# Two feed-forward networks in seven products: a stream of its own for the input combinations, and three plain tiles in the first network

## The chip, the cores and the metric

The kernel runs on one core of a Trainium2 chip. The metric is the device time of one execution in microseconds (us). The median of several runs is taken; lower is better. The engines are PE (TensorE, matmuls; PEld is its weight load), DVE (VectorE), ACT (ScalarE), POOL (GpSimd) and SP (SyncE, which here issues the transfers). Each runs its own instructions in a fixed order and waits on semaphores for the others.

## The reference, cut to what matters

A first block (a retention layer and a differential attention layer on 512 tokens of width 1024) is followed by a second one with two gated feed-forward networks of hidden width 2816 around a mixing layer. The change touches the two feed-forward networks only:

```python
def swiglu(x, w_gate, w_up, w_down):
    return (jax.nn.silu(x @ w_gate) * (x @ w_up)) @ w_down
...
def second_block(x, meta_tokens, ffn1_norm, ffn1_w_gate, ...):
    h = jnp.concatenate([meta, x], axis=1)          # 16 + 512 tokens
    for l in range(DEPTH_2):                        # DEPTH_2 = 1
        h = h + 0.5 * swiglu(rmsnorm_2(h, ffn1_norm[l]), ffn1_w_gate[l], ffn1_w_up[l], ffn1_w_down[l])
        u = rmsnorm_2(h, mix_norm[l])
        ...
        h = h + merged @ w_out[l]
        h = h + 0.5 * swiglu(rmsnorm_2(h, ffn2_norm[l]), ffn2_w_gate[l], ffn2_w_up[l], ffn2_w_down[l])
    return rmsnorm_2(h, final_norm)[:, N_META:]
```

The gain of the norm and the division by the root of the mean square are separate in the kernel: the matmuls take the input times the gain, and the factor of each token (called `bc`) is multiplied in afterwards.

## The kernel before, in words

All activations lie transposed in SBUF: `h[0..7]` are eight tiles of 128 channels by the tokens (528 in the first network, which also has 16 meta tokens; 512 in the second). Every float32 operand of a matmul is split into a rounded high part and a rest (`xh`, `xl`, `wh`, `wl`: ACT casts the high part, DVE subtracts it from the source), and every product is three matmuls, high by high, high by rest and rest by high (`mm3`).

A hidden tile is 128 of the 2816 hidden channels; there are 22 (`FT`). A tile needs a gate product and an up product, each over eight channel tiles. **Plain products** (tile 0 and 1, `FS` = 2) take the weights one tile `[128, 1024]` at a time from a stream (`plan`, then `raws`, two raw buffers, then `ready`; `stock` and `w`), three split pairs `wh`/`wl` at most. In the first network a plain gate or up tile is 48 matmuls of 264 columns (two token halves in two PSUM banks), so a plain hidden tile is 96.

**Seven products** (`Seven`, all other tiles) take a gate tile and an up tile together: split by halves of the channels they are a 2 by 2 matrix of blocks, the input split by halves of channels and tokens is another, and the 2 by 2 product is done with seven block products in place of eight. A block product is 12 matmuls (four channel tiles, three matmuls each), so a hidden tile is 84. For this there must be sums of weight blocks (`sums`, two on POOL and two on DVE per tile, from float32 copies that `load` fetches), splits of the seven weight operands (`split`, one half of a `wh`/`wl` pair each), and **combinations of the inputs**. `inputs` makes three of them once for each network: for each of four channel tiles ACT makes one product into a temporary (`e` in the first network, `o` in the second) and three casts, and DVE three combinations into the temporary and three rests into tiles named `at`; together 24 instructions on DVE and 16 on ACT. `first` overwrites the second token half of `x[0..3]` with a fourth combination just before the seven products start.

The program is recorded by generators (`Ctx.run`), which take turns by a model of time. Operations of DVE, ACT, POOL and SP are held back (`ops`) and written out per engine by earliest modelled start (`pump`), ties broken by rank; the matmuls stand in the order in which the generators make them. What comes out is one fixed order per engine. Two generators run in a network. `backbone` makes the matmuls: first the gate of tile 0, the up and the gate (three weight tiles), then the up of tile 1, then the seven products, then the down products (`wd`). `stats` closes the norm of the layer before (`arrive`), sums the squares, makes the token factor (matmul `pst`, DVE `rsv`, POOL power `rsr`, DVE `diag`, matmul `pbc`, ACT copy `bc`), finishes tile 0 and the gate of tile 1 (`up(0, ...)`, `R["t1"]`: DVE multiplies by `bc` into `t`, ACT applies Silu, DVE multiplies by the up product `mm`, both split into `hh`), and only then runs `seven.inputs`, with a rank that is three higher. `seven.feed` makes the loads, sums and splits of the next weight operands when there is room, from the up of tile 1 on. There are six PSUM banks for products (`mm`, taken in a ring), so the seventh bank wanted is free when the operation that reads the first is done: the banks of the up of tile 0 are read by `t<-mm,t`.

Of the kernel before, what the change touches and what calls it, by code (L numbers as in the profile page):

```python
# [11 lines left out]
F32R = mybir.dt.float32r  # L12
# [6 lines left out]
P = 128  # L19
D = 1024  # L20
KT = D // P
# [686 lines left out]

FS = 2


def ffn_items(which):
    it = []
    for f in range(FS):
        it += [(f"wg{which}", f, 0, 1024, None), (f"wu{which}", f, 0, 1024, None)]
    it.append(None)
    for m in range(KT):
        it += [(f"wd{which}", m, j * P, min(8, FT - j) * P, None) for j in range(0, FT, 8)]  # L720
    return it


class Seven:
# [9 lines left out]
    def __init__(self, c, which, pool, psp, entry, o, TH):  # L734
        self.c, self.which, self.pool, self.psp, self.entry, self.o, self.TH = c, which, pool, psp, entry, o, TH
        self.x = entry.x
        self.blocks = []
        for f in range(FS, FT + 1):
            for k, g in ((1, f), (4, f - 1), (2, f), (6, f), (3, f - 1), (7, f), (5, f)):
                if FS <= g < FT:  # L740
                    self.blocks.append((g, k))
        acts = [("load", FS), ("sums", FS)]
        for f, k in self.blocks:
            acts.append(("split", f, k))
            if (k == 4 or f == FS and k == 1) and f + 2 - (k == 1) < FT:
                acts.append(("load", f + 2 - (k == 1)))
            if k == 5 and f + 1 < FT:
                acts.append(("sums", f + 1))
        self.acts = acts
        self.g, self.u, self.a, self.ops, self.T = {}, {}, {}, {}, {}  # L750
        self.pair, self.made, self.used = None, 0, 0


    def at(self, j, shape, dtype):
        return self.pool.tile(shape, dtype, tag="more" if j == FT else f"hh{j}", name=self.c.nm("at"))

    def rank(self, f):
        c = self.c
# [9 lines left out]
    def feed(self):  # L768
        c = self.c
        while self.acts:  # L770
            it = self.acts[0]
            if it[0] == "load" and c.raws:
                return
            if it[0] == "split" and self.made % 2 == 0 and len(c.ready) + c.live + self.live() >= 3:
                return
            self.acts.pop(0)
            self.rank(lambda: getattr(self, it[0])(*it[1:]))
# [132 lines left out]
def ffn(c, which, after=None, out=None):  # L910
# [7 lines left out]
    with ExitStack() as es:  # L918
# [17 lines left out]
        def stats():  # L936
# [7 lines left out]
            yield from c.wait(lambda: c.rdy(R["bc"]) if "ps" in R else None)  # L944
            up(0, gate([R["t0"][:, i] for i in range(nb)]), R["ps"][1])
            R["t1"] = gate(R["ps"][2])
            c.mark(("first",))
            c.rank += 3
            yield from seven.inputs(temps)
            R["inputs"] = True  # L950

# [33 lines left out]
        def halve(*fs):  # L985
            for f in fs:
                h = pool.tile([P, W], F32R, tag=f"hh{f}", name=c.nm("hh"))
                l = pool.tile([P, W], F32R, tag=f"hl{f - 1}" if f > FS else "more", name=c.nm("hh"))
                c.split(h, l, hid[f])
                hh[f] = h, l  # L990


        def done(f, k, s):
            if not s.acts and c.plan and c.plan[0] is None:
                c.plan.pop(0)
                s.rank(lambda: halve(*range(2, 10)))
            if not s.acts:
                c.stock(s.live())
            if f == FT - 1 and k in (6, 7, 4):
# [5 lines left out]
        def backbone():  # L1005
# [26 lines left out]
                        c.stock(n - 1 - j)  # L1032
            R["ps"] = ps
            t = None
            for f in range(1, FS):
                if f > 1:
                    pg = MM()
                    yield from steps(pg, c.w(wg, f), x)
                    t = gate(pg)
                pu = MM()  # L1040
                w = c.w(wu, f)
# [46 lines left out]

        last = Final(c, pool, psp, out)
        if out is not None:  # L1090
            c.run(last.close(0), last.close(1), stats(), backbone())
            return
        c.run(stats(), backbone())


HR, DK, DV = 8, 128, 256
# [1741 lines left out]
```

## Time and profile before

| | |
|---|---|
| median of 3 runs | 2061.24 us (2056.95 to 2061.69) |
| the profiled execution's own time | 2056.42 us, span 2054.4 us |
| mean granted TensorE clock | 0.983 of full speed |
| PE busy | 1966.2 us (96%), 12509 matmuls |
| DVE, ACT, POOL busy | 1395.5, 981.1, 557.5 us |

The span is from the first to the last instruction; the execution's own time is a little more. The profile cuts the span in 40 slices of 51.4 us. PE is busy 8 tenths or more in all of them but slice 16, where the first network starts (7 tenths, the only slice whose granted clock reads 8 tenths and not 9); the second network starts in slice 34 (8 tenths between slices of 9). PE's row over time and the stretches around these two places are what there is to read.

### The profile page before, as it was taken

Reading aid. Unit: us, or ns where it says so; the run is one execution under the profiler, and the core shown is the slowest. Engines: PE = TensorE matmul, PEld = TensorE weight load, DVE = VectorE, ACT = ScalarE, POOL = GpSimd, SP = SyncE. Lnnn points to the kernel's source line nnn. Section 1 sums busy time; section 2 is a strip of 40 time slices with the busy share of each in tenths; the row PEclk is TensorE's granted clock in tenths of the full one; section 3 lists DMA queues with packets and bytes.
Section 4 is the critical chain, followed back from the end, with each engine's and each line's share of the span. In section 5 each row is a group of like instructions: output and inputs, shape, how many; then the busy total and the mean of one; then the engine's idle time right before and its main releaser. Section 6 shows DMA issues by size and latency. Waiting matters only on the chain. (4 is left out here: it accounts for less than half of the span.)

```text
span 2054.4 us, 32590 instructions
## 1 busy us (share of the span) xinstructions
PE 1966.2 (96%) x12509; PEld 1740.0 (85%) x12509; DVE 1395.5 (68%) x2736; ACT 981.1 (48%) x1987; POOL 557.5 (27%) x457
## 2 busy tenths in 40 slices
PE   8999999989999997999999989999999998999998
PEld 6888888877887886999999988976878787999887
DVE  6665564387677658999833476769786658999733
ACT  4444443256555555555622376643433345555521
POOL 3111120144443153222101243324544231222010
PEclk9999999999999998999999999999999999999999
DMA  4222221322111221333233411021021842333232
GB/s 158 74 82 83 77 78 62 123 72 72 62 63 62 72 83 47 108 100 109 78 94 95 154 47 37 32 83 61 32 73 33 271 153 67 109 116 101 82 98 78
DMA packets 67500, 178.80 MB, mean 87 GB/s; under 512 B 9040, under 2 KB 12240, under 8 KB 67344
## 3 DMA queue, kind: packets, MB, share of 16 engines
q1 hardware_dynamic: 65968, 175.54, 26.2%
q8 instruction: 98, 1.61, 0.3%
q10 hardware_dynamic: 1376, 1.18, 0.2%
q14 instruction: 58, 0.48, 0.1%
HBM read 166.21 MB, written 10.49 MB: 86 GB/s over the span
## 5 line engine op out<-in xcount | busy, mean ns | idle before, releaser
L415 PE MATMUL mm<-x,wh 128*128 128x264 f32 (+2 forms) x2896 | 701.1, 331 | 31.6 <-ACT x L254 15.2
L415 PEld LDWEIGHTS mm<-x,wh 128*128 128x128 f32 x2896 | 487.0, 192 | 75.7 <-ACT x L254 16.2
L415 PE MATMUL mm<-x,wl 128*128 128x264 f32 (+2 forms) x1448 | 476.3, 330 | 18.3 <-DVE wl L254 18.2
L254 ACT CAST wh<-raw 128x1024 fp32r<-128x1024 f32 (+2 forms) x307 | 271.4, 885 | 384.0 <-PE mm L415 244.1
L254 DVE TENSOR_TENSOR wl<-raw,wh 128x1024 fp32r<-128x1024 f32 (+2 forms) x265 | 271.7, 1025 | 184.6 <-ACT wh L254 183.4
L415 PEld LDWEIGHTS mm<-x,wl 128*128 128x128 f32 x1448 | 278.3, 193 | 41.0 <-DVE wl L254 19.2
L415 PE MATMUL mm<-hh,wh 128*128 128x264 f32 (+2 forms) x1100 | 227.0, 315 | 1.5 <-DVE hh L254 1.5
L254 POOL TENSOR_TENSOR acc<-acc,sq 128x512 f32<-128x512 f32 (+4 forms) x73 | 81.3, 1115 | 386.3 <-ACT sq L254 371.7
L415 PEld LDWEIGHTS mm<-hh,wh 128*128 128x128 f32 x1100 | 168.9, 188 | 17.5 <-DVE hh L254 4.4
L415 PE MATMUL mm<-at,wh 128*128 128x264 f32 (+1 forms) x960 | 178.6, 283 | 0.0
L415 PE MATMUL pvg<-wh,x 128*128 128x512 f32 x512 | 170.7, 397 | 0.0
L254 DVE TENSOR_TENSOR wl<-at,wh 128x512 fp32r<-128x512 f32 x200 | 157.0, 794 | 15.3 <-ACT wh L254 12.8
L254 ACT CAST wh<-at 128x512 fp32r<-128x512 f32 x200 | 120.0, 620 | 80.0 <-PE mm L415 70.7
L415 PEld LDWEIGHTS mm<-at,wh 128*128 128x128 f32 x960 | 149.1, 189 | 0.1
L415 PE MATMUL mm<-hh,wl 128*128 128x264 f32 (+2 forms) x550 | 144.6, 315 | 0.0
L415 PE MATMUL mm<-at,wl 128*128 128x264 f32 (+1 forms) x480 | 135.9, 283 | 0.8 <-DVE wl L254 0.8
L254 POOL TENSOR_TENSOR at<-at,raw 128x512 f32<-128x512 f32 x40 | 53.6, 1341 | 288.7 <-DVE wl L254 260.3
L254 POOL TENSOR_TENSOR wl<-raw,wh 128x1024 fp32r<-128x1024 f32 x42 | 101.6, 2422 | 108.1 <-ACT wh L254 102.9
L254 POOL TENSOR_TENSOR ra<-ra,rb 128x512 f32<-128x512 f32 x32 | 57.5, 1798 | 253.5 <-DVE rb L254 253.5
L415 PEld LDWEIGHTS pvg<-wh,x 128*128 128x128 f32 x512 | 96.3, 188 | 20.6
L415 PE MATMUL pvg<-wl,x 128*128 128x512 f32 x256 | 100.4, 392 | 0.0
L415 PEld LDWEIGHTS mm<-hh,wl 128*128 128x128 f32 x550 | 92.0, 188 | 5.5
(441 smaller groups left out, 3769.8 us busy)
## 6 DMA issues: line engine op xcount, KB each, us to landing
raw<-in_wg_dram SPq DMA_DIRECT2D x44, 512.0 KB, 4.1
at<-in_wu_dram SPq DMA_DIRECT2D x80, 256.0 KB, 3.1
raw<-in_w_mix_dram SPq DMA_DIRECT2D x36, 512.0 KB, 3.3
raw<-in_w_ret_vg_dram SPq DMA_DIRECT2D x32, 512.0 KB, 3.3
raw<-in_wd_dram SPq DMA_DIRECT2D x32, 512.0 KB, 3.6
raw<-in_w_dif_kq_dram SPq DMA_DIRECT2D x16, 512.0 KB, 3.2
raw<-in_w_ret_qk_dram SPq DMA_DIRECT2D x14, 512.0 KB, 3.3
raw<-in_w_ret_o_dram SPq DMA_DIRECT2D x13, 512.0 KB, 3.5
```

The lines of the kernel that those rows point to most:

```text
L254: p = Op(lambda: f(*a, **k), self.key, cost, tail, i, o, c.before(o), c.rank, c.t)
L415: return self.nc.tensor.matmul(out, lhsT, rhs, start=start, stop=stop, **kw)
```

## The change

`FS` becomes a number for each network: three plain tiles in the first (so tile 2 is made by plain products, and seven products make 19 tiles there), two as before in the second. `seven.inputs` leaves `stats` and becomes a generator of its own, `inputs`, between `stats` and `backbone` in the order of turns and of ranks. In the first network it starts when the token factor has been recorded as far as its tile `bc`, in the second when the inputs are there. The loads of the float32 weight copies after the first wait until `stats` is done with its part (`later`). The buffer that held a weight sum or copy in the place of tile 2's hidden values is, in the first network, that of the norm's sum (`acc`).

```diff
--- before.py
+++ after.py
@@ -708,12 +708,12 @@
 
 
 
-FS = 2
+FS = {1: 3, 2: 2}
 
 
 def ffn_items(which):
     it = []
-    for f in range(FS):
+    for f in range(FS[which]):
         it += [(f"wg{which}", f, 0, 1024, None), (f"wu{which}", f, 0, 1024, None)]
     it.append(None)
     for m in range(KT):
@@ -734,15 +734,19 @@
     def __init__(self, c, which, pool, psp, entry, o, TH):
         self.c, self.which, self.pool, self.psp, self.entry, self.o, self.TH = c, which, pool, psp, entry, o, TH
         self.x = entry.x
+
+        self.acc = "acc" if FS[which] > 2 else "hh2"
+        self.later = False
         self.blocks = []
-        for f in range(FS, FT + 1):
+        F0 = FS[which]
+        for f in range(F0, FT + 1):
             for k, g in ((1, f), (4, f - 1), (2, f), (6, f), (3, f - 1), (7, f), (5, f)):
-                if FS <= g < FT:
+                if F0 <= g < FT:
                     self.blocks.append((g, k))
-        acts = [("load", FS), ("sums", FS)]
+        acts = [("load", F0), ("sums", F0)]
         for f, k in self.blocks:
             acts.append(("split", f, k))
-            if (k == 4 or f == FS and k == 1) and f + 2 - (k == 1) < FT:
+            if (k == 4 or f == F0 and k == 1) and f + 2 - (k == 1) < FT:
                 acts.append(("load", f + 2 - (k == 1)))
             if k == 5 and f + 1 < FT:
                 acts.append(("sums", f + 1))
@@ -752,7 +756,7 @@
 
 
     def at(self, j, shape, dtype):
-        return self.pool.tile(shape, dtype, tag="more" if j == FT else f"hh{j}", name=self.c.nm("at"))
+        return self.pool.tile(shape, dtype, tag="more" if j == FT else self.acc if j == 2 else f"hh{j}", name=self.c.nm("at"))
 
     def rank(self, f):
         c = self.c
@@ -769,7 +773,7 @@
         c = self.c
         while self.acts:
             it = self.acts[0]
-            if it[0] == "load" and c.raws:
+            if it[0] == "load" and (c.raws or it[1] > FS[self.which] and not self.later):
                 return
             if it[0] == "split" and self.made % 2 == 0 and len(c.ready) + c.live + self.live() >= 3:
                 return
@@ -944,8 +948,12 @@
             yield from c.wait(lambda: c.rdy(R["bc"]) if "ps" in R else None)
             up(0, gate([R["t0"][:, i] for i in range(nb)]), R["ps"][1])
             R["t1"] = gate(R["ps"][2])
+            seven.later = True
             c.mark(("first",))
-            c.rank += 3
+
+        def inputs():
+            for k in range(KT):
+                yield from c.wait(lambda: entry.rdy(k), lambda: 0.0 if "bc" in R or not rest else None)
             yield from seven.inputs(temps)
             R["inputs"] = True
 
@@ -985,7 +993,7 @@
         def halve(*fs):
             for f in fs:
                 h = pool.tile([P, W], F32R, tag=f"hh{f}", name=c.nm("hh"))
-                l = pool.tile([P, W], F32R, tag=f"hl{f - 1}" if f > FS else "more", name=c.nm("hh"))
+                l = pool.tile([P, W], F32R, tag=f"hl{f - 1}" if f > FS[which] else "more", name=c.nm("hh"))
                 c.split(h, l, hid[f])
                 hh[f] = h, l
 
@@ -993,7 +1001,7 @@
         def done(f, k, s):
             if not s.acts and c.plan and c.plan[0] is None:
                 c.plan.pop(0)
-                s.rank(lambda: halve(*range(2, 10)))
+                s.rank(lambda: halve(*range(FS[which], 10)))
             if not s.acts:
                 c.stock(s.live())
             if f == FT - 1 and k in (6, 7, 4):
@@ -1032,10 +1040,13 @@
                         c.stock(n - 1 - j)
             R["ps"] = ps
             t = None
-            for f in range(1, FS):
+            for f in range(1, FS[which]):
                 if f > 1:
                     pg = MM()
-                    yield from steps(pg, c.w(wg, f), x)
+                    w = c.w(wg, f)
+                    for y in steps(pg, w, x):
+                        seven.feed()
+                        yield y
                     t = gate(pg)
                 pu = MM()
                 w = c.w(wu, f)
@@ -1088,9 +1099,9 @@
 
         last = Final(c, pool, psp, out)
         if out is not None:
-            c.run(last.close(0), last.close(1), stats(), backbone())
+            c.run(last.close(0), last.close(1), stats(), inputs(), backbone())
             return
-        c.run(stats(), backbone())
+        c.run(stats(), inputs(), backbone())
 
 
 HR, DK, DV = 8, 128, 256
```

In the program that comes out the first network has 12 more matmuls (one hidden tile of 84 in seven products is now 96), and DVE, ACT, POOL and SP have 9, 8, 2 and 1 instructions fewer. The order changes in two places, the starts of the two networks, and a little where the seven products of the first end.

PE, first network, where the up of tile 1 ends (`wl_7289` before, `wl_7291` now, are the rests of its weights; `x_...` are the split inputs, `mm_...` the banks). Before:

```order
L415 MATMUL mm_7321<-x_6978,wl_7289 128x264
L415 MATMUL mm_7322<-x_6978,wl_7289 128x264
L415 MATMUL mm_7454<-x_6964,wh_7330 128x264
L415 MATMUL mm_7454<-x_6965,wh_7330 128x264
L415 MATMUL mm_7454<-x_6964,wl_7331 128x264
```

Now:

```order
L415 MATMUL mm_7346<-x_6978,wl_7291 128x264
L415 MATMUL mm_7347<-x_6978,wl_7291 128x264
L415 MATMUL mm_7456<-x_6964,wh_7334 128x264
L415 MATMUL mm_7457<-x_6964,wh_7334 128x264
L415 MATMUL mm_7456<-x_6965,wh_7334 128x264
L415 MATMUL mm_7457<-x_6965,wh_7334 128x264
L415 MATMUL mm_7456<-x_6964,wl_7335 128x264
L415 MATMUL mm_7457<-x_6964,wl_7335 128x264
```

Before, the first of the seven products follows, with a half-width weight operand split from `raw_7323`; now the gate of tile 2 follows, in two banks, with the weights `wh_7334` and `wl_7335`, and after it the up of tile 2.

DVE, first network, from the last `diag` of the token factor (before) and from the first combinations behind the `diag`s (now). `e` and `at` are temporaries and results of `inputs`, `t` and `hh` belong to tile 0 and tile 1. Before:

```order
L254 TENSOR_SCALAR diag_7312<-ident,rsr_7301 128x128
L254 TENSOR_TENSOR at_7327<-at_7326,raw_7323 128x512
L254 TENSOR_TENSOR at_7329<-at_7327,raw_7323 128x512
L254 TENSOR_TENSOR wl_7331<-raw_7323,wh_7330 128x512
L254 TENSOR_TENSOR t_7411<-t_1366_7287,bc_7307 128x264 x2
L254 TENSOR_TENSOR t_7411<-mm_7061,t_7411 128x264
L254 TENSOR_TENSOR t_7411<-mm_7062,t_7411 128x264
L254 TENSOR_TENSOR t_7414<-mm_7063,bc_7307 128x264
L254 TENSOR_TENSOR t_7414<-mm_7064,bc_7307 128x264
L254 SCALAR_TENSOR_TENSOR e_7428<-h_84,par,e_7428 128x264
L254 SCALAR_TENSOR_TENSOR e_7427<-h_83,par,e_7427 128x264
L254 TENSOR_TENSOR hh_7413<-t_7411,hh_7412 128x528
```

Now:

```order
L254 SCALAR_TENSOR_TENSOR at_7327<-e_7329,at_7325 128x264
L254 SCALAR_TENSOR_TENSOR e_7331<-h_84,par,e_7331 128x264
L254 TENSOR_TENSOR at_7323<-e_7331,at_7321 128x264
L254 SCALAR_TENSOR_TENSOR at_7319<-e_7331,at_7317 128x264
L254 SCALAR_TENSOR_TENSOR e_7332<-h_85,par,e_7332 128x264
L254 SCALAR_TENSOR_TENSOR at_7327<-e_7331,at_7325 128x264
L254 TENSOR_TENSOR t_7441<-t_1367_7289,bc_7310 128x264 x2
L254 TENSOR_TENSOR t_7441<-mm_7063,t_7441 128x264
L254 TENSOR_TENSOR t_7441<-mm_7064,t_7441 128x264
L254 TENSOR_TENSOR wl_7335<-raw_7008,wh_7334 128x1024
L254 TENSOR_TENSOR hh_7443<-t_7441,hh_7442 128x528
L254 TENSOR_TENSOR t_7444<-mm_7065,bc_7310 128x264
```

Before, two weight sums, a rest and then the finishing of tile 0 followed the `diag`s, and the combinations came behind and among it; now nine combinations stand between the `diag`s and the finishing of tile 0 (four more stand ahead of the `diag`s), the rest `wl_7335` of the gate of tile 2 stands right behind the two `t<-mm,t`, and the other eleven combinations come after.

DVE, second network, around the rest of the weight operands of the first two of the seven products (`wl_17796` before, `wl_17837` now, one half each; `o` is the temporary of `inputs` and of `first`, `x` a result of `first`). Before:

```order
L254 SCALAR_TENSOR_TENSOR at_17817<-o_17819,at_17815 128x256
L254 TENSOR_TENSOR at_17794<-at_17792,raw_17788 128x512
L254 TENSOR_TENSOR x_17421<-o_17880,x_17420 128x256
L254 SCALAR_TENSOR_TENSOR o_17823<-h_17464,par,o_17823 128x256
L254 TENSOR_TENSOR wl_17796<-raw_17788,wh_17795 128x512
L254 SCALAR_TENSOR_TENSOR o_17823<-h_17333,par,o_17823 128x256
L254 TENSOR_TENSOR at_17814<-o_17823,at_17812 128x256
L254 SCALAR_TENSOR_TENSOR o_17823<-h_17464,par,o_17823 128x256
L254 SCALAR_TENSOR_TENSOR at_17810<-o_17823,at_17808 128x256
L254 SCALAR_TENSOR_TENSOR o_17882<-h_17334,par,o_17882 128x256
L254 SCALAR_TENSOR_TENSOR at_17818<-o_17823,at_17816 128x256
L254 TENSOR_TENSOR wl_17796<-raw_17788,wh_17795 128x512
```

Now:

```order
L254 TENSOR_TENSOR t_17839<-mm_17664,t_17839 128x512
L254 TENSOR_TENSOR hh_17841<-t_17839,hh_17840 128x512
L254 TENSOR_TENSOR at_17833<-at_17832,raw_17829 128x512
L254 TENSOR_TENSOR wl_17837<-raw_17829,wh_17836 128x512
L254 TENSOR_TENSOR t_17842<-mm_17828,t_17842 128x512
L254 SCALAR_TENSOR_TENSOR o_17892<-h_17316,par,o_17892 128x256
L254 SCALAR_TENSOR_TENSOR o_17893<-h_17317,par,o_17893 128x256
L254 TENSOR_TENSOR at_17835<-at_17833,raw_17829 128x512
L254 TENSOR_TENSOR hh_17889<-t_17842,hh_17888 128x512
L254 TENSOR_TENSOR x_17364<-o_17892,x_17363 128x256
L254 TENSOR_TENSOR x_17406<-o_17893,x_17405 128x256
L254 TENSOR_TENSOR wl_17837<-raw_17829,wh_17836 128x512
```

Before, the two halves stood among combinations; now all 24 combinations stand ahead of `t_17839`, and between the halves stand the product for tile 1 (`t_17842<-mm_17828`, which reads the last plain matmul's bank), half of `first`, a weight sum and a split.

## Rows read from the trace of the kernel before

**Rows 1.** The page's head and its first part: busy time, share, instructions
```profile
span 2054.4 us, 32590 instructions
...
PE 1966.2 (96%) x12509; PEld 1740.0 (85%) x12509; DVE 1395.5 (68%) x2736; ACT 981.1 (48%) x1987; POOL 557.5 (27%) x457
```
**Rows 2.** Busy time by stretch (first three: first network; last: second)
```profile
780.00:790.00 10.00, 7.24 (x56) 6.57 (x54) 7.75 (x18) 7.54 (x15) 1.56 (x2) 1.00 0.11 38
790.00:800.00 10.00, 1.79 (x8) 1.79 (x9) 10.00 (x26) 6.57 (x17) 0.00 (x0) 0.66 0.08 25
800.00:820.00 20.00, 16.18 (x103) 15.50 (x103) 17.58 (x29) 8.83 (x20) 6.55 (x4) 0.83 0.20 67
1710.00:1720.00 10.00, 3.50 (x15) 3.34 (x16) 9.49 (x24) 7.65 (x20) 0.00 (x0) 0.57 0.00 1
```
**Rows 3.** PE in order of time, first network (start, length, what, idle before)
```profile
784.88 0.41 PE L415 MATMUL mm<-x,wl 128*128 128x264 f32 x2
787.54 0.51 PE L415 MATMUL mm<-x,wh 128*128 128x264 f32 x2 [2.25 <-DVE t L254]
...
798.21 0.59 PE L415 MATMUL mm<-x,wl 128*128 128x264 f32 x1 [8.70 <-DVE wl L254]
...
813.89 0.40 PE L415 MATMUL mm<-at,wh 128*128 128x264 f32 x2
```
**Rows 4.** DVE in order of time, first network
```profile
776.38 1.22 DVE L254 TENSOR_TENSOR wl<-raw,wh 128x1024 fp32r<-128x1024 f32 x1 [1.96 <-ACT wh L254]
...
779.09 3.13 DVE L254 TENSOR_SCALAR diag<-ident,rsr 16x16 f32<-16x16 f32 x5 [1.36 <-POOL rsr L254]
782.15 1.40 DVE L254 TENSOR_TENSOR at<-at,raw 128x512 f32<-128x512 f32 x2
...
787.05 0.77 DVE L254 TENSOR_TENSOR t<-mm,t 128x264 f32<-128x264 f32 x2 [2.21 <-ACT t L254]
...
792.37 1.69 DVE L254 SCALAR_TENSOR_TENSOR e<-h,par,e 128x264 f32<-128x264 f32 x4
...
797.47 0.68 DVE L254 TENSOR_TENSOR wl<-raw,wh 128x512 fp32r<-128x512 f32 x1
```
**Rows 5.** PE in order of time, second network
```profile
1708.63 0.39 PE L415 MATMUL mm<-x,wh 128*128 128x256 f32 x2
1716.50 0.58 PE L415 MATMUL mm<-x,wl 128*128 128x256 f32 x1 [7.47 <-DVE wl L254]
...
1729.10 0.40 PE L415 MATMUL mm<-at,wh 128*128 128x256 f32 x2
```
**Rows 6.** DVE in order of time, second network
```profile
1687.74 1.56 DVE L254 TENSOR_TENSOR wl<-raw,wh 128x1024 fp32r<-128x1024 f32 x1 [0.70 <-ACT wh L254]
...
1691.00 1.91 DVE L254 TENSOR_SCALAR diag<-ident,rsr 128x128 f32<-128x128 f32 x4 [1.13 <-POOL rsr L254]
...
1703.29 0.69 DVE L254 TENSOR_TENSOR t<-mm,bc 128x512 f32<-128x512 f32 x1 [7.54 <-PE mm L415]
...
1708.83 0.69 DVE L254 TENSOR_TENSOR t<-mm,t 128x512 f32<-128x512 f32 x1 [0.47 <-PE mm L415]
```
**Rows 7.** PE, end of the seven-product stretch of the first network
```profile
1009.78 0.66 PE L415 MATMUL mm<-hh,wh 128*128 128x264 f32 x4
```
**Rows 8.** Busy time by stretch, steady part of the second network
```profile
1740.00:1800.00 60.00, 60.00 (x511) 60.00 (x511) 57.87 (x92) 32.65 (x66) 16.90 (x13) 1.00 0.34 109
```
**Rows 9.** ACT in order of time, first network
```profile
785.08 1.28 ACT L254 ACT_TABLE_LOAD   x1
786.38 0.64 ACT L254 ACTIVATE t<-t 128x528 f32<-128x528 f32 x1
```
**Rows 10.** Weight transfers issued in the first network, issue to landing
```profile
DMA to landing us min/median/max: 3.3/3.4/4.8
```
**Rows 11.** PE before the change's places: an idle piece
```profile
749.18 0.59 PE L415 MATMUL mm<-x,wh 128*128 128x264 f32 x1 [2.48 <-ACT x L254]
```
**Rows 12.** Busy time by stretch behind that piece (PEclk: granted clock)
```profile
749.00:759.00 10.00, 9.54 (x45) 9.24 (x46) 7.40 (x15) 5.85 (x15) 6.68 (x8) 0.50 0.46 154
```

## The prediction

> **What bounds the kernel now.** I read the page's first part, then the busy time by stretch, then PE and DVE in order of time where PE's share falls. PE is busy 96% of the span [rows 1], so time can come from few places. Two of them are the starts of the feed-forward networks. From 790 to 800 PE is busy 1.79 of 10 us while DVE is busy all 10, and from 1710 to 1720 PE 3.50 and DVE 9.49 [rows 2]. The reader should see there that PE waits for a DVE that is full, not for a transfer.
>
> First network: the up of tile 1 ends at 784.88 + 0.41 = 785.29. The first of the seven products waits 2.25 us for a bank (its releaser is the DVE product `t<-mm,t`), and the second one 8.70 us for the rest `wl` of its weights; the seventh block product starts at 813.89 [rows 3]. On DVE that `wl` came at 797.47, behind the combinations of `inputs`, such as the four of 1.69 us at 792.37 [rows 4].
>
> Second network: PE comes to the seven products at 1708.63 without a wait, then waits 7.47 us for a `wl`, and starts the seventh block product at 1729.10 [rows 5]. DVE had been idle for 7.54 us ahead of 1703.29 and began the combinations only after that [rows 6].
>
> What each start costs, in one number: from the seventh block product (813.89) to the first down product (1009.78, [rows 7]) PE makes 20 tiles less six blocks, 20 x 84 - 72 = 1608 matmuls, 195.89 us, 0.1218 us each, without an idle piece in PE's rows. Six blocks are then 72 x 0.1218 = 8.77 us, and the first network loses 813.89 - 785.29 - 8.77 = 19.8 us. In the second, 511 matmuls take 60 us [rows 8], a block of 12 is 1.41, and the loss is 1729.10 - 1708.63 - 6 x 1.41 = 12.0 us. Together 31.8 us is all that the change could touch.
>
> **The change part by part.**
>
> *The plain tile.* 96 matmuls for 84: +12 x 0.1218 = +1.46 us on PE. The plain tile is 96 x 0.1218 = 11.69 us of matmuls that need no combinations; one seven-product tile (10.23 us) falls away later, and with it a tile's DVE and ACT work, which lies beside PE and is worth nothing.
>
> *First network, the wait ahead of the gate of tile 2.* Its banks are those that `t<-mm,t` reads, and its `wl` stands right behind that pair on DVE. A combination into the temporary is priced at 1.69 / 4 = 0.42, a rest or any other 264-column pair at 0.77 / 2 = 0.39 [rows 4]. Four combinations ahead of the `diag`s take 3 x 0.42 + 0.39 = 1.65 us where DVE was idle 1.36 for POOL's power: the `diag`s end 0.3 later, at 779.09 + 3.13 + 0.3 = 782.5. Nine combinations follow, 4 x 0.42 + 5 x 0.39 = 3.6, to 786.1; the pair of `t<-t,bc` 0.77, to 786.9 (it ended before 785.08 so far). Then ACT's table load 1.28 and Silu 0.64 [rows 9], the pair `t<-mm,t` 0.77, the `wl` 1.22: 790.8. The first four matmuls of the gate (0.49) don't need the `wl`, so PE loses 790.8 - 0.49 - 785.29 = 5.0 us. From below: if the table load is done before `t` is there, 1.9 less, 3.1. From above: the casts and combinations call each other back and forth between ACT and DVE, and nine steps at some 0.5 us of idleness each add 4.5. I take 5.0, since DVE ran such a mixture from 790 to 800 without idling [rows 2].
>
> *The wait ahead of the up of tile 2.* DVE from 790.8: a split 0.70 (two 264-column halves, priced as 0.77 at most), a `t` pair 0.77, the next ten combinations 5 x 0.42 + 5 x 0.39 = 4.05, the `wl` 1.22: 797.5. The gate's 48 matmuls end at 785.29 + 5.0 + 5.85 = 796.1, and the `wl` is wanted at 796.6: 0.9 us of wait, 0 to 5 by the same two reasons. Ahead of one of the casts ACT must also wait for the weights of tile 3, a transfer that cannot start before the `wl` of 790.8 frees its buffer; it lands 3.4 us later (4.8 at most, [rows 10]), before 796, so it is hidden. If it were slower, the `wl` would be late by as much.
>
> *The first seven products.* The up of tile 2 ends at 796.1 + 0.9 + 5.85 = 802.9. From 797.5 DVE has one rest 0.39, two pairs 1.54, two weight sums of 1.40 / 2 [rows 4], a split 0.70 and two `wl` of 0.68: 5.4 us, to 802.9. So they are there just as PE arrives; 0.5 us for what follows (`first` stands among the next operands), 0 to 3.
>
> *The clock.* Behind an idle piece of 2.48 us [rows 11] PE ran 10 us at a granted clock of 0.50, the 1.2 GHz level [rows 12]; behind the 2.25 us wait at 785 it kept the full level until the 8.70 us wait. After 5.0 us of waiting I expect the low level. The Trainium skill (TensorE: Matmul & The Clock Gate, "HAM oscillation") says the same, that idle gaps bring the clock down and work brings it back; the trace agrees. The loss is half of the slow stretch: 4.9 us if as long as in [rows 12], nothing if the clock holds. Part of it covers the 0.9 us wait and lets DVE get ahead. I take 2.0.
>
> First network: lost 5.0 + 0.9 + 0.5 + 2.0 = 8.4 instead of 19.8, and +1.46: a gain of 10.0 us.
>
> *Second network.* From the end of the gate's `wl` (1687.74 + 1.56 = 1689.3, [rows 6]) DVE now has 24 combinations, 12 x 0.42 + 12 x 0.39 = 9.7, the `diag`s 1.91 and one `wl` of 1.22: 12.9 us, to 1702.2, ahead of the 1703.29 at which it must be free for tile 1. So the combinations are hidden under the plain products, and if ACT makes them 2 us longer, there are still 5 us until the first seven products want anything. But the second half of their first weight operand stands behind `t<-mm,t` for tile 1, which waits for PE's last plain matmul and started at 1708.83: 0.69 + two temporaries 0.84 + sum 0.70 + split 0.69 + two rests 0.77 + `wl` 0.68 = 4.4, to 1713.2. PE reaches it at 1708.63 + 1.41 + 0.24 = 1710.3 and waits 2.9 us. The next operands come 0.7 us behind one another, faster than a block. With 1.0 for the clock (0 to 2.5) and 0.3 for a later `pbc`, the loss is 4.2 instead of 12.0: a gain of 7.8 us.
>
> *`later`, the buffer `acc`, fewer instructions.* The loads held back have their buffers free no sooner than before, the steady order of the transfers is as it was, and `acc` is free once the norm's sum is read, ahead of the load that wants it: nothing, unless a transfer turns up late in each tile (a rival below).
>
> **Sum.** 10.0 + 7.8 = 17.8 us. The profiled execution took 2056.42; that gives 2038.6. The three runs shown took 2056.95, 2061.24 and 2061.69, on average 3.5 more than the profiled one, and the time asked for is a median of such runs: 2038.6 + 3.5 = 2042.
>
> **The rivals.**
>
> *The waits all but go.* The clock holds and the table load is early: the first network loses 3.1 + 0.9 and gains 19.8 - 1.46 - 4.0 = 14.4, the second loses 2.9 and gains 9.1: 23.5, 2036. For it: 2.25 us at 785 did not cost the clock. Against: ACT has two casts of `inputs` and a weight cast ahead of the table load.
>
> *The waits move.* ACT and DVE in turns add the 4.5 us to the first wait and the low clock costs its 4.9: the first network loses 5.0 + 4.5 + 0.9 + 0.5 + 4.9 = 15.8 and gains 19.8 - 1.5 - 15.8 = 2.5, the second, with 2.5 for the clock, gains 12.0 - 2.9 - 0.3 - 2.5 = 6.3. Sum 8.8, 2051. For it: a combination, its cast and its rest hang on one another. Against: two channel tiles are interleaved, and DVE was full in such a stretch.
>
> *Nothing is gained.* The waits ahead of tile 2 and in the second network are as long as those removed. What is left is the plain tile, 2056.42 + 1.46 = 2057.9, with the 3.5 above 2061.4. This is what the Trainium skill's rule to work on the most contended engine first would give (Perfetto Trace Analysis, "Identifying the Most-Contended Engine"): PE is that engine by [rows 1], and it gets 12 more matmuls. Against it are the rows in which PE stands idle beside a full DVE [rows 2].
>
> *Slower.* DVE is busy 57.87 of 60 us in the steady stretch of the second network [rows 8]. If the held-back loads left the weight sums one step late in every tile, PE would wait there 39 times. From (17.8 + 6) / 39 = 0.6 us per tile on the kernel would be slower by more than can be told; at 0.7 us it is 2042 + 39 x 0.7 = 2069. Against: in the order of the transfers the pattern of a tile is as before.
>
> **Numbers.** The forecast 0.58, the waits all but go 0.16, they move 0.14, nothing gained 0.08, slower 0.04. The difference that a measurement of this kernel can tell is about 0.3%, 6 us. Faster: 0.58 + 0.16 + most of 0.14, 0.86; same 0.10; slower 0.04. The range reaches from 2034, just below the best case, to 2052, just above the case in which the waits move, and leaves out the other two.
>
> **What would show it.** Right: PE's next wait behind the up of tile 1 is some 5 us and names DVE `wl` (or `t`), about 1 us ahead of the up of tile 2, none of 8 us; in the second network one wait of about 3 us, with a `wl` as its releaser, inside the second block product, and DVE busy under the plain products where it was idle. Wrong: a wait over 8 us ahead of the gate of tile 2, a low clock for over 10 us, or waits that come back in every tile of the steady stretch.

## The result and the profile after

The changed kernel takes 2043.24 us, the median of five runs (2040.94 to 2050.54), against 2061.24 (2056.95 to 2065.91) for the kernel before: ratio (of the means) 0.9922, interval 0.9896 to 0.9947. The profiled execution took 2040.94 us, its span is 2039.0.

PE in order of time in the changed kernel, first network, as in [rows 3], with the first down product last:
```profile
782.32 0.41 PE L415 MATMUL mm<-x,wl 128*128 128x264 f32 x2
785.42 1.36 PE L415 MATMUL mm<-x,wh 128*128 128x264 f32 x4 [2.70 <-DVE t L254]
786.89 0.81 PE L415 MATMUL mm<-x,wl 128*128 128x264 f32 x2
...
794.39 0.66 PE L415 MATMUL mm<-x,wh 128*128 128x264 f32 x4
...
809.05 0.39 PE L415 MATMUL mm<-x,wh 128*128 128x264 f32 x1 [1.89 <-DVE x L254]
...
811.22 0.40 PE L415 MATMUL mm<-at,wh 128*128 128x264 f32 x2
...
997.51 0.65 PE L415 MATMUL mm<-hh,wh 128*128 128x264 f32 x4
```
The up of tile 1 ends at 782.73, the gate of tile 2 waits 2.70 us, the up follows at 794.39 without a wait, and the seventh block product starts at 811.22. The 8.70 us wait of [rows 3] is gone. Lost by the prediction's count: 811.22 - 782.73 - 11.69 - 8.77 = 8.0 us.

The second network, as in [rows 5]:
```profile
1698.48 0.39 PE L415 MATMUL mm<-x,wh 128*128 128x256 f32 x2
...
1702.69 0.46 PE L415 MATMUL mm<-x,wl 128*128 128x256 f32 x1 [2.40 <-DVE wl L254]
...
1711.21 0.40 PE L415 MATMUL mm<-at,wh 128*128 128x256 f32 x2
...
1902.00 0.62 PE L415 MATMUL mm<-hh,wh 128*128 128x512 f32 x2
```
One wait of 2.40 us, in place of 7.47 and 1.54 us ones; lost 1711.21 - 1698.48 - 6 x 1.41 = 4.3 us. The second of the waits before, and the first down product there:
```profile
1726.97 0.39 PE L415 MATMUL mm<-x,wh 128*128 128x256 f32 x1 [1.54 <-DVE x L254]
...
1918.76 0.63 PE L415 MATMUL mm<-hh,wh 128*128 128x512 f32 x2
```

Busy time by stretch, as in [rows 2] and [rows 8] (PE, PEld, DVE, ACT, POOL, granted clock):
```profile
785.00:795.00 10.00, 9.47 (x53) 9.12 (x54) 10.00 (x21) 5.11 (x11) 1.99 (x1) 0.68 0.17 54
1700.00:1710.00 10.00, 7.60 (x51) 7.39 (x50) 10.00 (x18) 6.53 (x16) 3.04 (x2) 0.83 0.17 55
1740.00:1800.00 60.00, 60.00 (x508) 60.00 (x507) 56.43 (x92) 33.12 (x68) 16.70 (x12) 1.00 0.34 109
```
PE is now busy where it stood idle, though for part of the time at the lower level of its clock (1.2 GHz), and DVE is as full as it was.

To compare kernels I use two lengths that fold in everything a network's start costs: **first**, from the end of the up of tile 1 to the first down product; **second**, from the first of the seven products to the first down product. Before: 1009.78 - 785.29 = 224.5 and 1918.76 - 1708.63 = 210.1 us ([rows 3, 5, 7] and the row above). After: 214.8 and 203.5. The gains are 9.7 and 6.6 us.

### The profile page after: what moved, and what is told of

Its sections match the earlier page's. It is cut to its first block, busy times and chain, and to the rows that moved or that the text cites. A ratio compares the mean times of both kernels' runs of the same rounds, so it can differ in the third digit from the quotient of the medians.

```text
span 2039.0 us, 32593 instructions
## 1 busy us (share of the span) xinstructions
PE 1968.7 (97%) x12521; PEld 1741.7 (85%) x12521; DVE 1387.8 (68%) x2727; ACT 979.2 (48%) x1979; POOL 556.8 (27%) x455
## 5 line engine op out<-in xcount | busy, mean ns | idle before, releaser
L415 PE MATMUL mm<-at,wh 128*128 128x256 f32 (+1 forms) x936 | 174.4, 283 | 0.0
L254 DVE TENSOR_TENSOR wl<-at,wh 128x512 fp32r<-128x512 f32 x195 | 150.4, 782 | 14.1 <-ACT wh L254 11.9
L415 PE MATMUL mm<-at,wl 128*128 128x256 f32 (+1 forms) x468 | 132.7, 284 | 0.0
```

What stands on the lines that cost most here:

```text
L254: p = Op(lambda: f(*a, **k), self.key, cost, tail, i, o, c.before(o), c.rank, c.t)
L415: return self.nc.tensor.matmul(out, lhsT, rhs, start=start, stop=stop, **kw)
```

## The experiments

All ten runs, each timed beside the kernel before on the same chip. The third length is the stretch between the networks, from the one's first down product to the other's seven products, at which no edit is aimed.

| run | first, us | second, us | between, us | ratio to before | interval |
|---|---|---|---|---|---|
| before | 224.5 | 210.1 | 698.9 | 1 | |
| the change | 214.8 | 203.5 | 701.0 | 0.9922 | 0.9896 to 0.9947 |
| the change again | 215.0 | 202.8 | 696.0 | 0.9918 | 0.9894 to 0.9942 |
| 1 stream alone | 217.9 | 203.5 | 700.2 | 0.9936 | 0.9915 to 0.9958 |
| 2 third tile alone | 219.5 | 210.1 | 703.5 | 0.9965 | 0.9947 to 0.9983 |
| 3 second network only | 225.0 | 202.8 | 698.7 | 0.9970 | 0.9952 to 0.9988 |
| 4 table early | 212.5 | 203.5 | 697.8 | 0.9909 | 0.9888 to 0.9930 |
| 5 splits early | 215.1 | 203.6 | 696.4 | 0.9930 | 0.9910 to 0.9949 |
| 6 sums of tile 4 on DVE | 215.1 | 203.5 | 697.8 | 0.9942 | 0.9919 to 0.9965 |
| 7 three edits | 213.5 | 201.2 | 702.9 | 0.9923 | 0.9903 to 0.9942 |
| 8 sums of tile 3 on DVE | 214.6 | 203.3 | 703.5 | 0.9910 | 0.9887 to 0.9933 |
| 9 as 7, and 8 | 213.6 | 201.1 | 703.8 | 0.9900 | 0.9876 to 0.9923 |

**The change again**, nothing altered. 

> The changed kernel once more, with nothing altered, as the measure of how much its pieces move from one execution to the next. Own theory: from the end of the up of tile 1 to the first down product 214.8 us within 1.5 (wait of 2.7 to 3 us ahead of the gate of tile 2, and the length of the low clock behind it varies), in the second network from the first of the seven products to the first down product 203.5 within 0.8; the unchanged stretch between the networks, 698.9 and 701.0 us in the two profiles so far, again within 3 us to either side; ratio 0.992 (0.990 to 0.9945). Rival, the 2.1 and 1.4 us that the unchanged stretches lost in the first profile are of the change: they come again to 0.3 us.


The starts repeat to 0.2 and 0.7 us. The stretch between them moves over 7.8 us in these twelve profiles, and in its last 60 us, where the second network begins, PE waits for nothing but 0.74 us for a `diag` in run 8; so the 2.1 us there need not be of the change. The 1.4 us behind the second network's first down product did come again (2054.4 - 1918.76 = 135.6 before, 2039.0 - 1902.00 = 137.0, then 137.1), and the rival stays open for them. The other profiles lean towards it: this piece is 136.3 to 137.1 us in all that have the stream in the second network, and 136.0 in run 2, which has it not. Differences of a few us between runs 4 to 9 are therefore read from the two starts, not from the ratios.

**1. The stream alone.** 

> The changed kernel with two plain tiles in both networks, so only the stream of its own is left in the first one. Own theory: the second network keeps its gain (6.6 to 7.8 us), the first one gains only about 6 of its 9.7, because 15 of the 24 combinations on DVE are still to be done when the plain products end and no plain tile lies over them: a wait of about 8 us ahead of the third block product (the first that reads a combination), 13 to 14 us lost in place of 19.8. Ratio to the kernel before 0.994 (0.9925 to 0.9955). Rival, the third tile alone does it: nothing gained in the first network, ratio 0.9965. Rival, the third tile does nothing: 0.992 as with the whole change.


```diff
-FS = {1: 3, 2: 2}
+FS = {1: 2, 2: 2}
```
PE's waits in the first network:
```profile
783.90 0.48 PE L415 MATMUL mm<-x,wh 128*128 128x264 f32 x2 [1.50 <-DVE t L254]
793.87 0.59 PE L415 MATMUL mm<-x,wl 128*128 128x264 f32 x1 [9.48 <-DVE wl L254]
```
The first network gains 6.6 us, the second 6.6, as expected. The long wait came two blocks earlier than I had it: in the first block product, after its first two matmuls. The `wl` of that block stands behind the combinations. Behind that wait no other follows.

**2. The third tile alone.** 

> The changed kernel with three plain tiles in the first network, but the combinations at the end of the stream for the norm, behind its mark and three ranks later, as in the kernel before. Own theory: the first network keeps nearly all of its gain (about 9 of 9.7 us), since the 11.7 us plain tile covers most of the 19 us of DVE work; the second one falls back to a wait of 7 to 8 us for a wl and gains nothing: ratio 0.9955 (0.9945 to 0.9965). Rival, the stream is needed in the first network too: 5 us or less there, ratio 0.9976 or more.


```diff
             c.mark(("first",))
+            c.rank += 3
+            yield from seven.inputs(temps)
+            R["inputs"] = True
 
         def inputs():
-            for k in range(KT):
...
+            return
+            yield
```
```profile
790.41 1.36 PE L415 MATMUL mm<-x,wh 128*128 128x264 f32 x4 [2.69 <-DVE t L254]
809.85 0.39 PE L415 MATMUL mm<-x,wl 128*128 128x264 f32 x1 [4.36 <-DVE wl L254]
```
The second network gains nothing, as both expected. In the first my theory fell: 5.0 us gained, not 9. The 11.7 us tile covers only part of DVE's work, and 4.36 us of waiting for the same `wl`, that of the first block product, are left. Together the parts bring 9.7, apart 6.6 and 5.0: each removes some of the same wait.

**3. The second network only.** 

> The kernel before with the stream of its own in the second network alone (the first as before, two plain tiles). Own theory: the gains of the networks add up, so this is 6.6 to 7.8 us: ratio 0.9965 (0.9955 to 0.997), one wait of 2 to 3 us for a wl in the second block product there, and the first network with its 2.3 and 8.7 us waits. Rival, the difference comes from the first network alone or from run to run: 0.999 to 1.001.


```diff
             c.mark(("first",))
+            if which == 1:
+                c.rank += 3
+                yield from seven.inputs(temps)
+                R["inputs"] = True
 
         def inputs():
+            if which == 1:
+                return
```
(with two plain tiles in both.) The second network gains 7.3 us, the first nothing: the two gains are separate. One part of the expectation fell: the first network does not show its 2.3 and 8.7 us waits. `later` and the turns of the generators stand in it too, and they bring the `wl` of the second block product forward; PE then waits for the combinations instead:
```profile
791.58 0.39 PE L415 MATMUL mm<-x,wl 128*128 128x264 f32 x1 [3.59 <-DVE wl L254]
...
796.13 0.59 PE L415 MATMUL mm<-at,wh 128*128 128x264 f32 x1 [2.48 <-ACT at L254]
```
With the smaller waits behind these the start is as long as before (225.0 against 224.5). That speaks for the work on DVE and ACT as what costs there, and not the place of one `wl`.

**4. The table early.** 

> The changed kernel, and in the first network ACT loads its Silu table ahead of the norm's statistics by a one-element activation; the scheduler also puts the wl of the gate of tile 2 ahead of the t pair. Own theory: the chain through the table load set the wait of 2.70 + 0.97 us ahead of the gate of tile 2; without 1.28 us of load and with the wl ready, 1.5 to 2.2 us are left of 3.7, and if the clock then holds, 3 more: the first network loses 4 to 6 us in place of 8.0, ratio 0.9905 to 0.9915. Rival, the wait moves (to the up of tile 2, whose wl is now behind more combinations, or to the fifth block product): 7.5 us lost or more, ratio 0.992 as for the whole change.


```diff
+            if which == 1:
+                c.table_for(AF.Silu)
             r = c.rstd(pool, psp, acc, tts, D)
```
PE's wait ahead of the gate of tile 2, and the stretches around it:
```profile
788.28 0.97 PE L415 MATMUL mm<-x,wh 128*128 128x264 f32 x4 [2.02 <-DVE t L254]
```
```profile
780.00:790.00 10.00, 7.98 (x63) 7.45 (x62) 9.29 (x23) 6.77 (x15) 1.56 (x3) 1.00 0.42 152
790.00:800.00 10.00, 10.00 (x84) 10.00 (x84) 10.00 (x22) 6.29 (x14) 1.36 (x1) 1.00 0.23 80
```
The wait falls from 2.70 to 2.02 us, the first matmul that needs the `wl` follows 0.8 us later in place of 1.5 (on DVE the `wl` now stands ahead of the `t` pair, and is ready), and the clock holds. Only about half of the 1.28 us of the table load arrive: the `wl` now delays `t`, and DVE waits 0.57 us for the first `e`, which ACT makes behind the load. Four waits of 0.2 to 0.4 us for a `wl` come in the seven products, and the 1.89 us one is gone; 2.3 us are gained on the change. The chain norm, `t`, table load, Silu, `t<-mm,t` did set that wait.

**5. The splits early.** 

> The changed kernel, in the second network the casts and rests of the first two weight operands (four halves) at the rank of the plain work, not five behind it, which puts them ahead of the product t<-mm,t of tile 1 on DVE. Own theory: the wait of 2.40 us in the second block product was that place on DVE alone and is gone, but the rests of x for the fifth block product now stand behind a product that waits for PE, and PE waits about 2.5 us there: the second network stays within 1 us of 203.5, ratio 0.992. Rival, the wait goes and nothing takes its place: 200 to 201 us, ratio 0.9905. Rival, the place on DVE did not matter (the weights come late): 2.4 us of wait where it was.


```diff
-            self.rank(lambda: getattr(self, it[0])(*it[1:]))
+            f = lambda: getattr(self, it[0])(*it[1:])
+            f() if it[0] == "split" and self.made < 4 and self.which == 2 else self.rank(f)
```
```profile
1708.06 0.58 PE L415 MATMUL mm<-x,wh 128*128 128x256 f32 x1 [1.46 <-DVE x L254]
```
The 2.40 us wait is gone, and three of 0.29, 0.16 and 1.46 us take its place, in the fifth block product as expected. Nothing is gained.

**6. The sums of tile 4 on DVE.** 

> The changed kernel, in the first network the two weight sums that POOL makes for tile 4 (the second of the seven-product tiles) are made by DVE instead. Own theory: the pairs of 1.88 and 1.91 us on DVE at 803 and 806 were held by POOL's two sums that run at the same time (a pair takes 0.76 to 0.89 elsewhere); with DVE's own two sums (0.68 each) partly ahead, the x for the fifth block product come 1.4 to 2.1 us earlier and its wait of 1.89 us shrinks to 0.5 or less: 212.5 to 213.5 us in place of 214.8. Rival, the pairs are slow for another reason (the queue of ACT, a semaphore): they stay at 1.9 us, and the wait grows by 0.7 to 1.4 us. Ratio 0.9915 or 0.9925, too near to tell; the trace decides.


```diff
+        own = nc.vector if self.which == 1 and f == 4 else nc.gpsimd
...
-            ((nc.gpsimd, u[0], u[1]), (nc.vector, a[0], g[:, :512]), (nc.gpsimd, u[0], g[:, :512]), (nc.vector, a[1], g[:, 512:]))
+            ((own, u[0], u[1]), (nc.vector, a[0], g[:, :512]), (own, u[0], g[:, :512]), (nc.vector, a[1], g[:, 512:]))
```
DVE and POOL in the changed kernel, where two pairs are slow:
```profile
803.05 1.88 DVE L254 TENSOR_TENSOR x<-e,x 128x264 fp32r<-128x264 f32 x2
...
805.79 1.91 DVE L254 SCALAR_TENSOR_TENSOR e<-h,par,e 128x264 f32<-128x264 f32 x2
```
```profile
802.65 1.64 POOL L254 TENSOR_TENSOR at<-at,raw 128x512 f32<-128x512 f32 x1 [10.38 <-DVE wl L254]
806.00 1.41 POOL L254 TENSOR_TENSOR at<-at,at 128x512 f32<-128x512 f32 x1 [1.71 <-ACT pt L254]
```
The same pairs on DVE with those sums taken from POOL, and PE's wait:
```profile
806.71 0.77 DVE L254 TENSOR_TENSOR x<-e,x 128x264 fp32r<-128x264 f32 x2
...
808.34 0.89 DVE L254 SCALAR_TENSOR_TENSOR e<-h,par,e 128x264 f32<-128x264 f32 x2
```
```profile
813.67 0.39 PE L415 MATMUL mm<-x,wl 128*128 128x264 f32 x1 [1.97 <-DVE wl L254]
```
A pair loses 1.0 to 1.1 us to one sum of POOL, which is the theory, and the wait for `x` in the fifth block product is gone. But as long a wait took its place, in the sixth: it is for the `wl` of tile 4's first operand, which moved behind DVE's own sums. Right mechanism, no gain.

**7. Three edits.** 

> Three edits at once: the table load of the earlier run, the first four half operands of the second network ahead, and there also the four temporaries and rests of the modified input halves ahead of all else. Own theory: the first network as with the table load alone (212.5 us, 2.3 less than the changed kernel), in the second one neither the wait of 2.40 us nor one in the fifth block product, and no low clock: 200 to 201 us in place of 203.5; together 5 us less than the changed kernel, ratio 0.9895 (0.988 to 0.991). Rival, the two waits exchange places again: the second network at 203 us or more, ratio 0.991 to 0.992.


Runs 4 and 5 together, and `first` ahead of all else in the second network:
```diff
+        r, c.rank = c.rank, -1 if self.which == 2 else c.rank
         self.first(temps)
+        c.rank = r
```
```profile
1709.77 0.38 PE L415 MATMUL mm<-x,wl 128*128 128x256 f32 x1 [1.31 <-DVE wl L254]
```
The second network gains 2.3 us on the change, with 1.31 us of waiting left, later than before, and a clock that holds. The first gains 1.3 us where run 4 gained 2.3, with the same order of work: its clock was at 0.85 from 790 to 800, in run 4 at 1.00. The two starts are 3.6 us shorter together; the ratio shows none of it.

**8. The sums of tile 3 on DVE.** 

> The changed kernel, in the first network the two weight sums that POOL makes for tile 3 (the first of the seven-product tiles) are made by DVE, which gets them behind the t of tile 2; DVE's order up to there is the same. Own theory: the five diag products took 2.04 us because one of POOL's sums ran beside them (0.99 us without one, 3.13 with two in the kernel before); they fall to 1.0 us, the wait ahead of the gate of tile 2 from 2.70 to 1.65 us, the clock holds as behind the waits of 2.02 us, and about 1 us comes back as a wait in the second block product, whose weights now stand behind the two sums: 211.5 us (210.5 to 213) from the end of the up of tile 1 to the first down product, in place of 214.8 to 215.1. Rival, POOL has nothing to do with it: the diags stay at 2.0 us and the first network gets longer by the two sums, 215.5 to 216.5.


The edit of run 6 with `f == 3`. The five `diag` products with one sum of POOL beside them, in the changed kernel, then without:
```profile
776.78 2.04 DVE L254 TENSOR_SCALAR diag<-ident,rsr 16x16 f32<-16x16 f32 x5
```
```profile
783.63 1.00 DVE L254 TENSOR_SCALAR diag<-ident,rsr 16x16 f32<-16x16 f32 x5
```
In [rows 4] they took 3.13, with two sums beside them. So one sum costs DVE 1.0 to 1.1 us here too. The rest of the theory fell: the wait ahead of the gate only went from 2.70 to 2.30 us, since the next link stood right behind. The `t` pair in the changed kernel, then ACT and DVE in this run:
```profile
782.08 0.77 DVE L254 TENSOR_TENSOR t<-t,bc 128x264 f32<-128x264 f32 x2
```
```profile
786.72 0.38 ACT L254 COPY bc<-pbc 128x264 f32<-128x264 f32 x1 [0.48 <-PE pbc L415]
```
```profile
787.55 0.49 DVE L254 SCALAR_TENSOR_TENSOR e<-h,par,e 128x264 f32<-128x264 f32 x1 [0.33 <-ACT e L254]
...
788.49 0.77 DVE L254 TENSOR_TENSOR t<-t,bc 128x264 f32<-128x264 f32 x2
```
The pair starts 788.49 - 783.63 = 4.9 us after the first `diag`, in place of 782.08 - 776.78 = 5.3: 0.4 of the 1.0 us is left. The rest went into DVE's waits among the combinations for ACT, whose next product `e` stands behind a copy of `bc`, and that copy now waits for PE's `pbc`. A wait of 0.50 us for the `wl` follows the 2.30, and the clock fell (0.83 from 790 to 800).

**9. All of it.** 

> The three edits at once of the earlier run, and the sums of tile 3 on DVE. Own theory: the wait ahead of the gate of tile 2 falls to about 1 us, the clock holds: 211 to 212.5 us in the first network, 201.2 in the second as before: 5 to 6 us less than the changed kernel in the two starts, ratio 0.989 (0.987 to 0.991), so that the difference to the changed kernel is at the edge of what can be told. Rival, what is taken from the wait comes back behind it, in the seven products, since DVE has two more sums: 213 us or more, and ratio 0.991 to 0.9925.


```profile
782.65 0.97 PE L415 MATMUL mm<-x,wh 128*128 128x264 f32 x4 [0.98 <-DVE t L254]
798.99 0.59 PE L415 MATMUL mm<-x,wl 128*128 128x264 f32 x1 [3.87 <-DVE wl L254]
```
The rival, in the first network: the first wait is down to 0.98 us, and 3.87 us come back in the first block product, whose `wl` stands behind DVE's own sums. The ratio is the lowest of the ten, but its interval holds the ratio of the change: that this version is faster than the change was not shown.

## Why the prediction was right

It forecast 2042 us (2034 to 2052) and the median is 2043.24. Point by point:

- *What bounds the kernel.* Right. The change touched the 31.8 us that PE lost at the two starts, and 19.5 of them are gone by the prediction's count (31.8 - 8.0 - 4.3), at the price of 1.46 for the plain tile.
- *The wait ahead of the gate of tile 2.* 5.0 us forecast; PE lost 786.89 - 0.49 - 782.73 = 3.7. The mechanism was right (`t`, table load, Silu, `t<-mm,t`, `wl`, each right behind the other), the size 1.3 too long, mostly the `diag`s: priced at 3.13 us, they took 2.04, because only one of POOL's two sums now runs beside them (run 8).

The table load stands right behind the `t` pair, as assumed:
```profile
782.97 1.28 ACT L254 ACT_TABLE_LOAD   x1
784.26 0.64 ACT L254 ACTIVATE t<-t 128x528 f32<-128x528 f32 x1
```
- *The wait ahead of the up of tile 2.* 0.9 us forecast, none measured, within its 0 to 5.
- *The seven products.* 0.5 us forecast, 1.89 measured, within 0 to 3. The term that was missed is POOL: its two sums held DVE for 2.2 us there (run 6). That the wait would go without this was not shown, since in run 6 DVE made the sums itself.
- *The clock.* 2.0 us forecast. The gate of tile 2 took 794.39 - 785.42 = 8.97 us in place of 5.85, of which 0.97 are the late `wl` counted above: 2.15 us.
- *First network.* 3.7 + 1.9 + 2.15 and 0.3 in small pieces make the 8.0 us lost (forecast 8.4). The gain is 10.3 us by the seventh block product and 9.7 by the first down product (forecast 10.0). Of the 0.6 us between, 0.4 is a wait at the end of the seven products, in every profile with three plain tiles and in none with two:
```profile
995.95 0.51 PE L415 MATMUL mm<-x,wh 128*128 128x264 f32 x2 [0.38 <-DVE hid L254]
```
 That the sum came out so near is luck in part: errors of 1.3 us (first wait) and 1.4 us (seven products) had opposite signs.
- *Second network.* The combinations lie under the plain products, as forecast: DVE, idle for 7.54 us ahead of its `t<-mm,bc` in [rows 6], is idle there for 0.16 us now. The wait was 2.40 us where 2.9 was forecast, in the place forecast, with the `wl` behind `t<-mm,t`:
```profile
1693.13 0.69 DVE L254 TENSOR_TENSOR t<-mm,bc 128x512 f32<-128x512 f32 x1 [0.16 <-PE mm L415]
...
1698.68 0.69 DVE L254 TENSOR_TENSOR t<-mm,t 128x512 f32<-128x512 f32 x1 [1.68 <-PE mm L415]
...
1701.95 0.68 DVE L254 TENSOR_TENSOR wl<-raw,wh 128x512 fp32r<-128x512 f32 x1
```
 Beside the wait 4.3 - 2.40 = 1.9 us were lost, where 1.0 (0 to 2.5) was forecast for the clock. Not all of it is the clock's. In the repetition the clock held, and there 1708.93 - 1697.02 - 8.46 = 3.45 us were lost, 0.7 of them beside the waits of 2.40 and 0.36 us:
```profile
1697.02 0.39 PE L415 MATMUL mm<-x,wh 128*128 128x256 f32 x2
...
1707.65 0.39 PE L415 MATMUL mm<-x,wl 128*128 128x256 f32 x1 [0.36 <-DVE wl L254]
...
1708.93 0.40 PE L415 MATMUL mm<-at,wh 128*128 128x256 f32 x2
```
 So about 1.2 us are left for the low clock, near the forecast. Up to the seventh block product the gain is 7.7 us (7.8 forecast); 1.1 of it is lost again along the following 190 us, where no row shows a wait and PE makes 508 matmuls in 60 us in place of 511 [rows 8]. This is of the change: from the seventh block product to the first down product it is 190.8 to 191.0 us in every profile with the stream in the second network, 189.7 before and 189.6 in run 2, and the loss is even, 9.97 us for a tile's 84 matmuls in place of 9.91. The prediction had no term for it. Why is open.
- *`later`, `acc`.* Nothing forecast; no wait in the steady stretch of either network answers to them. `later` stands without the stream and the plain tile in the first network of run 3, where nothing was gained; `acc` was not tried apart.
- *The sum.* The profiled execution went from 2056.42 to 2040.94, 15.5 us, where 17.8 was forecast. The starts give 9.7 + 6.6; up to the end of the up of tile 1 the changed kernel's profile is 2.6 us ahead, then 2.1 and 1.4 behind in the stretches after the networks. The first two of these move so from run to run (the end of the up of tile 1 lies at 781.7 to 789.5 us in the twelve profiles; ahead of it [rows 12] show the lower clock for 10 us in the kernel before). The 3.5 us from profile to runs came out as 2.3, which took back part of the error. So the 1.2 us between forecast and median are luck in part: the gain is 18.0 us by the medians, 16.1 by the means of the runs and 15.5 by the profiles.
- *The rivals.* The waits did not all but go: the table load was not early, and the clock fell. Nor did they grow as in "the waits move": 3.7 us were lost ahead of the gate of tile 2, not 9.5. "Nothing is gained" does not hold: PE has 12 matmuls more in the profile (x12521 for x12509 in [rows 1]) and is done sooner. The prediction took this rival from the Trainium skill (Perfetto Trace Analysis, "Identifying the Most-Contended Engine"), which says to optimize the most contended engine first. That rule by itself forecasts no such thing: what was gained is idle time of PE, the most contended engine, so the trace does not speak against it. The late loads are absent.

## What to carry to other kernels

Where a full helper engine starves the busy one, moving its work under work that doesn't need it pays, and so does putting more such work over it, but the two overlap: 6.6 and 5.0 us alone made 9.7 together. After that each wait has the next link right behind it: what runs 5, 6 and 9 took from one wait came back at another place. Compare such edits by the length of the stretch they touch, not by the whole run, when unchanged code moves by more than they bring.

## What the hardware showed that was not expected

**POOL holds DVE, and DVE POOL.** One weight sum on POOL lengthened DVE's work beside it by 1.0 to 1.1 us wherever the two were taken apart: five `diag`s 1.00, 2.04 and 3.13 us with none, one and two sums (run 8, the change, before), a pair 0.77 and 1.88. In these rows a DVE operation that starts beside the sum ends after it. Not every DVE operation does, and the two can change places. In the changed kernel `t<-mm,pt`, which has one input in PSUM, keeps its 0.43 us beside a sum, and the `wl` behind it takes 1.41 us in place of 0.68:
```profile
814.31 1.30 POOL L254 TENSOR_TENSOR at<-at,raw 128x512 f32<-128x512 f32 x1 [6.90 <-DVE wl L254]
```
```profile
814.39 0.43 DVE L254 TENSOR_TENSOR t<-mm,pt 128x264 f32<-128x264 f32 x1 [0.16 <-PE mm L415]
814.74 1.41 DVE L254 TENSOR_TENSOR wl<-at,wh 128x512 fp32r<-128x512 f32 x1
```
In run 4 it was POOL's sum that took 4.46 us in place of 1.3, while the DVE operations beside it kept their lengths:
```profile
806.94 4.46 POOL L254 TENSOR_TENSOR at<-at,raw 128x512 f32<-128x512 f32 x1 [15.58 <-DVE wl L254]
```
The Trainium skill (SBUF — State Buffer, "Who interferes with whom") says that the two engines share a pair of ports as an exclusive lock, so that the later one waits for the whole operation, where the DVE operation has two inputs in SBUF or runs in a two-port mode; the trace agrees.

**The clock after the same wait.** Behind the wait of 2.4 us in the second network the granted clock fell in five of the seven profiles that have it and held in two. One of these is the change again, where the stretch behind it reads
```profile
1700.00:1710.00 10.00, 8.40 (x68) 8.19 (x69) 10.00 (x18) 6.17 (x15) 3.05 (x2) 1.00 0.24 75
```
against 0.83 above, with the same code. The fall costs 0.7 us in all (203.5 against 202.8); where the clock holds, a wait of 0.36 us for a `wl` follows that the slower products hide. In the first network it fell behind all five waits of 2.7 us. Behind one of 2.02 us it held, and behind one of 2.03 us, in the same code up to there, it was down to 0.85 in 790 to 800.
